# Stick-breaking attention: scaled queries split once, scores read by ScalarE, norms stored in columns

## Chip, cores and metric

The kernel runs on one core of a Trainium2 chip. A core has TensorE (PE; its loading of weights is listed apart as PEld), VectorE (DVE), ScalarE (ACT), GpSimd (POOL) and SyncE (SP), whose queue issues the DMAs here. The metric is the device time of one execution in microseconds; the median of the runs counts. All data are float32, and products of full accuracy are made from halves: every operand is split into a high part in the format fp32r and a rest (low part), and three matmuls, high by high, high by low and low by high, add up in PSUM.

## The reference

The model has two layers of width 1024 over 1024 positions: a gated DeltaNet layer and a layer with stick-breaking attention, each followed by a SwiGLU network and a gated embedding. The change lies in the attention alone. Its core:

```python
def sb_mixer(hn, k_sh, v_sh, w_q, q_norm, w_out):
    q = (hn @ w_q).reshape(b_, s_, SB_HEADS, SB_HEAD_DIM)
    q = (rms_norm(q, q_norm) * (SB_HEAD_DIM ** -0.5)).transpose(0, 2, 1, 3)
    o = stick_breaking(q, k_sh, v_sh)
    return o.transpose(0, 2, 1, 3).reshape(b_, s_, SB_WIDTH) @ w_out

def stick_breaking(q, k, v):
    ...
        z = jnp.einsum('bhtd,bhsd->bhts', q[:, :, t0:t1], k[:, :, :t1])
        mask = s_idx < t_idx
        log_not = jnp.where(mask, jax.nn.log_sigmoid(-z), 0.0)
        suffix = lax.cumsum(log_not, axis=3, reverse=True) - log_not
        log_w = jnp.where(mask, jax.nn.log_sigmoid(z) + suffix, -jnp.inf)
        outs.append(jnp.einsum('bhts,bhsd->bhtd', jnp.exp(log_w), v[:, :, :t1]))
```

There are 8 heads of 128 dimensions. The keys, too, are RMS-normalised per head and position.

## The kernel before

**Stages.** `whole` (line 2010) records DeltaNet, its tail, `attention` (line 1739) and its tail, one after the other. Activations lie transposed: 128 features on the partitions, 512 positions (a half, `hf` or `T`, 0 or 1) in the free dimension.

**The attention's work.** The dense part, `sb_dense` (line 1794), makes for each head the projections k, v and q of both halves, 24 matmuls each into a PSUM tile `mm`. After each one `sb_features` (line 1817) turns it into operands: ScalarE copies the tile to `ev` (two buffers); TensorE transposes it into a PSUM tile `z` (two buffers, shared with the scores); for k and q ScalarE sums the squares from there into `ms` (`msk`, `msq`), four numbers on each partition, DVE scales them, and GpSimd raises them to the power -0.5 (`rk`, `rq`, 128 x 4). DVE multiplies the keys by the gains `kq`, casts `ev` to the high part (`kh`, `qh`) and subtracts for the low part (`kl`, `ql`). The inverse norms of the keys stay as `rk`, one per partition of a score tile. Those of the queries are needed along the free dimension: TensorE transposes `rq` (4 rows of 128), DVE copies it to `rr`, a DMA stores it to `rD` in DRAM, and another loads it as a row into all 128 partitions, `rw`.

**The chains.** `sb_chains` (line 1875) spawns three generators for each head and half. `front` makes a score tile for each block of 128 keys, from the last block to the first (4 blocks in half 0, 8 in half 1; diagonal blocks have 128 to 512 columns): three matmuls into `z`, then DVE takes it out to `zs` and multiplies by `rk` and `rw` in one instruction (line 1908); ScalarE makes Abs, Exp and Ln into `t`; DVE adds the positive part; on diagonal blocks GpSimd masks (`select`); DVE splits `t` into `sh` and `sl`. `back` multiplies these by triangles of ones into the running sum `c`, and DVE subtracts it from `zs`. `weights` takes the exponential (ScalarE) and splits into `wh` and `wl`; `out` multiplies by the values `vh`, `vl` into `o`. At a half's end `o` is copied to an `ev` buffer, split and put to DRAM (`oD`), or straight into the operand tiles `x` of the output projection where those are there already (`spill`, line 1184).

**What sets the order.** Nothing on the chip does: every engine works through its instructions in the order in which they were recorded. The order comes from a planner, `Flow` (line 83), which runs all generators against a clock of its own with a cost for each instruction (line 114), buffers as slots (`slots`, `take`, `give`) and priorities (chains before features before dense work); the dense matmuls are its filling where no chain is ready. Its cost for a DMA (line 194) counts runs shorter than 128 elements as more data; its rule for GpSimd and DVE at their shared port (line 136) leaves the power out (line 143). A feature of q may be made up to four halves ahead of its use (line 1800). After the heads follows the output projection, `out_first` (line 1221) for half 0: its first two tiles are made together, all heads but the last first, then the last head. It is recorded into the last heads' chains as soon as `load_o` of half 0 is there.

Of the kernel before, what the change touches and what calls it, by code (L numbers as in the profile page):

```python
# [8 lines left out]
F32 = mybir.dt.float32  # L9
F32R = mybir.dt.float32r  # L10
AF = mybir.ActivationFunctionType
ALU = mybir.AluOpType
# [3 lines left out]
P = 128  # L16
# [3 lines left out]
H = 8  # L20
HW = 512
# [248 lines left out]
class Net:  # L270
    def __init__(self, tc, io, cp, act, wp, mm, dr):
# [7 lines left out]
        self.direct = set()  # L279
        self.early = []  # L280
        self.lead = 9.0
        self.slots = {tag: [0.0] * n for tag, n in {"mm": 2, "dn": 4, "u": 8, "tp": 3, "st": 2, "ca": 2, "zz": 1, "ou": 1, "vf": 2, "sg": 2, "xe": 2, "z": 2, "ev": 2, "pj": 3, "po": 1, "y": 3, "c": 2, "zs": 4, "t": 2, "hv": 2, "sl": 4, "wl": 2, "sh": 4, "wh": 2}.items()}
        self.banks = None
        nc = self.nc
        self.cst = cp.tile([P, 5, P], F32, name="cst")
# [1453 lines left out]
    def attention(self):  # L1739
        nc, io, tc, flow = self.nc, self.io, self.tc, self.flow  # L1740
        with ExitStack() as es:
            sp = es.enter_context(tc.tile_pool(name="as", bufs=2, reuse_waits="tile"))
            pp = es.enter_context(tc.tile_pool(name="ap", bufs=2, space=PSUM, reuse_waits="tile"))
# [23 lines left out]
                yield from self.normed(("n3", 1), self.r1, lambda k: hs[k], None, lambda: self.t(sp, "sh", bufs=4), "sh", lambda: self.give("zs"))  # L1767

            flow.spawn(second(), 0)
            for h in range(H):  # L1770
                for T in range(2):
                    self.sb_chains(h, T)
            yield from self.sb_dense()
            flow.spawn(self.late(), 4)
            yield lambda: ("tile", ("ol", 1, 0)) in flow.at
# [41 lines left out]
    def sb_features(self, n, h, hf, ps):  # L1817
        nc, sp, pp, flow, st = self.nc, self.sp, self.pp, self.flow, self.ast[h]
        yield from self.take("ev")
        yield  # L1820
        ev = self.t(sp, "ev")
        nc.scalar.copy(ev, ps)
        self.give("mm")
        a, b = (self.t(sp, n + p, dt=F32R, bufs=4 if n == "q" else 5) for p in "hl")
        st[n, hf] = (a, b)
        yield
        yield from self.take("z")
        pt = self.t(pp, "z")
        for c in range(4):
            nc.tensor.transpose(pt[:, c * P : (c + 1) * P], ev[:, c * P : (c + 1) * P], self.ident)  # L1830
        yield
        if n == "v":
            nc.scalar.copy(a, pt)
            yield
            nc.vector.tensor_tensor(b, pt, a.bitcast(F32), op=ALU.subtract)
            self.give("z", "ev")
            flow.mark(("ap", n, h, hf))
            return
        ms = self.t(sp, "ms" + n, (P, 4))
        for c in range(4):  # L1840
            nc.scalar.activation(self.junk, pt[:, c * P : (c + 1) * P], AF.Square, accum_out=ms[:, c : c + 1])
        self.give("z")
        src = ev
        if n == "k":
            nc.vector.tensor_scalar(ev, ev, self.kq, None, op0=ALU.mult)
        nc.vector.tensor_copy(a, ev)
        yield
        nc.vector.tensor_tensor(b, ev, a.bitcast(F32), op=ALU.subtract)
        yield
        self.give("ev")  # L1850
        nc.vector.tensor_scalar(ms, ms, 1.0 / P, EPS, op0=ALU.mult, op1=ALU.add)
        yield
        r = self.t(sp, "r" + n, (P, 4), bufs=4)
        nc.gpsimd.tensor_tensor(r, ms, self.nhalf[:, :4], op=ALU.pow)
        yield
        if n == "k":
            st["rk", hf] = r
            flow.mark(("ap", n, h, hf))
            return
        yield from self.take("z")  # L1860
        pr = self.t(pp, "z")
        nc.tensor.transpose(pr[:4, :P], r, self.ident)
        yield
        rr = self.t(sp, "rr", (4, P))
        nc.vector.tensor_copy(rr, pr[:4, :P])
        self.give("z")
        yield
        nc.sync.dma_start(self.rD[2 * h + hf], rr)
        yield
        rq = self.t(sp, "rw", bufs=3)  # L1870
        nc.sync.dma_start(rq, self.rD[2 * h + hf].rearrange("c p -> (c p)").unsqueeze(0).to_broadcast([P, HW]))
        st["rq", hf] = rq
        flow.mark(("ap", n, h, hf))

    def sb_chains(self, h, T):


        nc, sp, pp, flow, st = self.nc, self.sp, self.pp, self.flow, self.ast[h]
# [11 lines left out]
        def front():  # L1890
            yield lambda: all(flow.done(("ap", n, h, i)) for i in range(T + 1) for n in "kvq")
            yield from self.take("c")
            qh, ql = st["q", T]
            rq = st["rq", T]
            for j in range(jt, -1, -1):
                cols, dg, diag, js, n = geom(j)
                yield lambda: cnt["front"] - cnt["back"] < 3
# [5 lines left out]
                self.mmul(pz[:, cols], kh[:, js], ql[:, cols], False, False)  # L1903
                self.mmul(pz[:, cols], kl[:, js], qh[:, cols], False, True)
                yield
                yield from self.take("zs")
                z = self.t(sp, "zs", bufs=4)
                nc.vector.scalar_tensor_tensor(z[:, cols], pz[:, cols], rk[:, j % 4 : j % 4 + 1], rq[:, cols], op0=ALU.mult, op1=ALU.mult)
                self.give("z")
                yield  # L1910
                yield from self.take("t")
                t = self.t(sp, "t", bufs=2)
                nc.scalar.activation(t[:, cols], z[:, cols], AF.Abs)
                nc.scalar.activation(t[:, cols], t[:, cols], AF.Exp, scale=-1.0)
                nc.scalar.activation(t[:, cols], t[:, cols], AF.Ln, bias=1.0)
                yield
# [58 lines left out]
        def out():  # L1975
            po = None
# [13 lines left out]
            self.hdone[h] += 1  # L1990
            yield from self.take("ev")
            yield
            oe = self.t(sp, "ev")
            nc.scalar.copy(oe, po)
            yield
            if ("tile", ("ol", 1, T)) in flow.at:
# [95 lines left out]
```

## Time and profile before

| | |
|---|---|
| time, median of 3 runs | 2829.93 us (2829.88 to 2833.13) |
| the profiled execution | 2831.9 us, span 2830.2 us |
| granted TensorE clock, mean | 0.997 |
| attention, first transpose of `ev` to last `o` | 1523.4 to 2018 us |

The profile is that of one execution. Its timeline counts from the span's start; "busy" is the time in which an engine worked, "x" a number of instructions. All instructions carry the line of a helper (L64), so groups are told by their tiles, written output<-inputs without buffer numbers. The matmuls' ends are modelled and overlap the next start.

### The profile page before, as it was taken

The page shows a single profiled execution, that of the slowest core. Times are in us where ns is not written, and L with a number is a line of the kernel's source. Part 1 is how long each engine was busy: PE and PEld are TensorE (multiplying, and loading weights), DVE is VectorE, ACT ScalarE, POOL GpSimd, SP SyncE. Part 2 cuts the span into 40 slices and gives each one's busy share as a digit, 9 for nine tenths or more (in the row PEclk, how much of TensorE's full clock was granted, in tenths as well). Part 3 has the DMA queues.
Part 4 walks back from the last instruction along what each step waited for, and adds up shares of the span by engine and source line. Part 5 has one row for each costly group of instructions (what it writes and reads, how often), then busy time and mean ns, then how long its engine had stood idle before and what let it go on. Part 6 is the DMA issues. An engine that isn't in the chain of part 4 may idle for free.

```text
span 2830.2 us, 37782 instructions
## 1 busy us (share of the span) xinstructions
PE 2759.6 (98%) x13203; PEld 2271.2 (80%) x13203; DVE 2026.8 (72%) x3861; ACT 1276.1 (45%) x2567; POOL 881.6 (31%) x742
## 2 busy tenths in 40 slices
PE   8899999999999999999999999999999999999999
PEld 7687777888878888888877778887777888888777
DVE  7777787784685655477867888998796655557783
ACT  6646545553443433322345566666453333422241
POOL 0101110110056666543201222221027666734400
PEclk9999999999999999999999999999999999999999
DMA  4312221227624444587432111114524444477622
GB/s 144 130 60 78 68 73 63 77 84 247 218 79 157 145 151 149 198 313 305 152 129 95 49 46 64 60 46 160 178 91 143 155 143 155 152 287 284 266 97 104
DMA packets 165631, 395.89 MB, mean 140 GB/s; under 512 B 34048, under 2 KB 35392, under 8 KB 155968
## 3 DMA queue, kind: packets, MB, share of 16 engines
q1 hardware_dynamic: 165440, 393.48, 39.1%
q8 instruction: 104, 1.70, 0.3%
q14 instruction: 87, 0.71, 0.1%
HBM read 274.29 MB, written 119.11 MB: 139 GB/s over the span
## 4 chain that ended last, share of the span: by engine, by line
PE 74%; DVE 14%; ACT 2%; issue 2%; DMA 2%; POOL 1%; SPq 0%; POOLq 0%; DVEq 0%; ACTq 0%
PE dn L64 37%; PE mm L64 27%; PE tp L64 3%; PE z L64 2%; PE c L64 2%; PE o L64 2%; DVE yr L64 1%; DVE x L64 1%; DVE ca L64 1%; DVE wlo L64 1%; DVE xr L64 1%; DVE u L64 1%; DVE v L64 1%; DVE hx L64 1%; PE po L64 1%
## 5 line engine op out<-in xcount | busy, mean ns | idle before, releaser
L64 PE MATMUL mm<-x,whi 128*128 128x512 f32 x2880 | 951.2, 400 | 12.8 <-DVE x L64 7.9
L64 PEld LDWEIGHTS mm<-x,whi 128*128 128x128 f32 x2880 | 533.6, 189 | 115.0 <-DVE x L64 13.8
L64 PE MATMUL mm<-x,wlo 128*128 128x512 f32 x1440 | 573.7, 398 | 0.0
L64 PE MATMUL dn<-x,whi 128*128 128x512 f32 x1776 | 549.2, 390 | 2.1 <-DVE x L64 0.9
L64 POOL TENSOR_TENSOR wlo<-raw,whi 128x512 fp32r<-128x512 f32 x236 | 346.0, 1487 | 442.0 <-ACT whi L64 368.1
L64 ACT CAST whi<-raw 128x1024 fp32r<-128x1024 f32 x231 | 242.9, 1052 | 445.3 <-DVE raw L64 258.4
L64 PEld LDWEIGHTS dn<-x,whi 128*128 128x128 f32 x1776 | 333.1, 188 | 74.7 <-DVE x L64 3.3
L64 PE MATMUL dn<-x,wlo 128*128 128x512 f32 x888 | 345.8, 389 | 0.0
L64 PEld LDWEIGHTS mm<-x,wlo 128*128 128x128 f32 x1440 | 271.6, 189 | 47.5 <-issue 0.2
L64 PE MATMUL dn<-hx,whi 128*128 128x512 f32 x864 | 267.6, 391 | 0.5 <-DVE hx L64 0.4
L64 DVE TENSOR_TENSOR tt<-u,tt 128x512 fp32r<-128x512 f32 x140 | 144.4, 1031 | 82.0 <-ACT tt L64 82.0
L64 PEld LDWEIGHTS dn<-x,wlo 128*128 128x128 f32 x888 | 166.7, 188 | 34.4
L64 PEld LDWEIGHTS dn<-hx,whi 128*128 128x128 f32 x864 | 162.8, 189 | 35.5 <-DVE hx L64 1.3
L64 DVE TENSOR_TENSOR v<-v,dn 128x512 f32<-128x512 f32 x112 | 76.6, 685 | 155.2 <-PE dn L64 154.6
L64 DVE TENSOR_TENSOR wlo<-raw,whi 128x512 fp32r<-128x512 f32 x226 | 155.5, 698 | 33.9 <-ACT whi L64 33.8
L64 PE MATMUL dn<-hx,wlo 128*128 128x512 f32 x432 | 169.2, 392 | 3.4 <-POOL wlo L64 3.4
L64 POOL TENSOR_TENSOR wlo<-sw,whi 128x512 fp32r<-128x512 f32 x102 | 144.4, 1433 | 0.8 <-ACT whi L64 0.8
L64 ACT CAST tt<-u 128x512 fp32r<-128x512 f32 x140 | 85.1, 620 | 125.4 <-DMA yD<-tt 102.3
L64 DVE TENSOR_TENSOR E<-E,dn 128x512 f32<-128x512 f32 x132 | 90.0, 684 | 69.2 <-PE dn L64 66.9
L64 POOL TENSOR_TENSOR rs<-ms,nhalf 128x4 f32<-128x4 f32 x11 | 12.4, 1123 | 330.0 <-DVE ms L64 260.5
L64 DVE SCALAR_TENSOR_TENSOR ca<-xe,conv,ca 128x512 f32<-128x512 f32 x144 | 107.6, 749 | 6.2 <-ACT ca L64 6.0
L64 PE MATMUL dn<-y,whi 128*128 128x512 f32 x352 | 108.4, 389 | 0.0
(333 smaller groups left out, 5136.5 us busy)
## 6 DMA issues: line engine op xcount, KB each, us to landing
yD<-tt SPq DMA_DIRECT2D x296, 256.0 KB
x<-yD SPq DMA_DIRECT2D x58, 1024.0 KB
raw<-f_s SPq DMA_DIRECT2D x84, 512.0 KB
raw<-d_s SPq DMA_DIRECT2D x40, 512.0 KB
raw<-w_in SPq DMA_DIRECT2D x33, 512.0 KB
hx<-yD SPq DMA_DIRECT2D x16, 1024.0 KB
x<-oD SPq DMA_DIRECT2D x27, 512.0 KB
raw<-g_out SPq DMA_DIRECT2D x16, 512.0 KB
```

What stands on the lines that cost most here:

```text
L64: r = issue(*args, **kw)
```

## The change

Four edits, all in the attention.

1. The keys' gains are no longer multiplied in on DVE. ScalarE makes the high part with the gain as its scale, and DVE the low part in one instruction, `ev` times gain less high part, placed behind the power.
2. The queries' inverse norms are multiplied into `ev` before it is split. For that the norms are stored straight from `rq` (128 x 4), word by word into columns, and loaded as a row as before; the transpose on TensorE and the copy to `rr` are gone. DVE multiplies by the row, ScalarE casts, DVE subtracts. `ev` is held until then and has three buffers in place of two; `rw` has two in place of three.
3. A score tile is read from PSUM by ScalarE, twice: Abs with `rk` as scale into `t`, and Copy with that scale into `zs`. DVE's instruction is gone.
4. The last chains are spawned in another order: half 0 of head 7 ahead of half 1 of head 6.

```diff
@@ slots
-"z": 2, "ev": 2, "pj": 3
+"z": 2, "ev": 3, "pj": 3
@@ attention
-            for h in range(H):
-                for T in range(2):
-                    self.sb_chains(h, T)
+            chains = [(h, T) for h in range(H) for T in range(2)]
+            for h, T in chains[:-3] + [chains[-2], chains[-3], chains[-1]]:
+                self.sb_chains(h, T)
@@ sb_features
         self.give("z")
-        src = ev
         if n == "k":
-            nc.vector.tensor_scalar(ev, ev, self.kq, None, op0=ALU.mult)
-        nc.vector.tensor_copy(a, ev)
-        yield
-        nc.vector.tensor_tensor(b, ev, a.bitcast(F32), op=ALU.subtract)
-        yield
-        self.give("ev")
+            nc.scalar.activation(a, ev, AF.Copy, scale=self.kq)
+        yield
         nc.vector.tensor_scalar(ms, ms, 1.0 / P, EPS, op0=ALU.mult, op1=ALU.add)
         yield
         r = self.t(sp, "r" + n, (P, 4), bufs=4)
         nc.gpsimd.tensor_tensor(r, ms, self.nhalf[:, :4], op=ALU.pow)
-        yield
         if n == "k":
+            nc.vector.scalar_tensor_tensor(b, ev, self.kq, a.bitcast(F32), op0=ALU.mult, op1=ALU.subtract)
+            self.give("ev")
+            yield
             st["rk", hf] = r
             flow.mark(("ap", n, h, hf))
             return
-        yield from self.take("z")
-        pr = self.t(pp, "z")
-        nc.tensor.transpose(pr[:4, :P], r, self.ident)
-        yield
-        rr = self.t(sp, "rr", (4, P))
-        nc.vector.tensor_copy(rr, pr[:4, :P])
-        self.give("z")
-        yield
-        nc.sync.dma_start(self.rD[2 * h + hf], rr)
-        yield
-        rq = self.t(sp, "rw", bufs=3)
+        yield
+        nc.sync.dma_start(self.rD[2 * h + hf].rearrange("c p -> p c"), r)
+        yield
+        rq = self.t(sp, "rw")
         nc.sync.dma_start(rq, self.rD[2 * h + hf].rearrange("c p -> (c p)").unsqueeze(0).to_broadcast([P, HW]))
-        st["rq", hf] = rq
+        yield
+        nc.vector.tensor_tensor(ev, ev, rq, op=ALU.mult)
+        yield
+        nc.scalar.copy(a, ev)
+        yield
+        nc.vector.tensor_tensor(b, ev, a.bitcast(F32), op=ALU.subtract)
+        self.give("ev")
         flow.mark(("ap", n, h, hf))
@@ front
+                yield from self.take("t")
                 yield from self.take("zs")
+                t = self.t(sp, "t", bufs=2)
                 z = self.t(sp, "zs", bufs=4)
-                nc.vector.scalar_tensor_tensor(z[:, cols], pz[:, cols], rk[:, j % 4 : j % 4 + 1], rq[:, cols], op0=ALU.mult, op1=ALU.mult)
+                rj = rk[:, j % 4 : j % 4 + 1]
+                nc.scalar.activation(t[:, cols], pz[:, cols], AF.Abs, scale=rj)
+                nc.scalar.activation(z[:, cols], pz[:, cols], AF.Copy, scale=rj)
                 self.give("z")
-                yield
-                yield from self.take("t")
-                t = self.t(sp, "t", bufs=2)
-                nc.scalar.activation(t[:, cols], z[:, cols], AF.Abs)
                 nc.scalar.activation(t[:, cols], t[:, cols], AF.Exp, scale=-1.0)
```

Since the planner sets the order from its costs, every engine's order in the attention changes with this. Three places follow (the numbers in the names tell tiles apart and differ between the two kernels).

DVE behind the sum of squares of a query, half 0, in a middle head, before: the rows up to the instruction that first reads a score tile.

```order
L64 TENSOR_SCALAR msq_16790<-msq_16790 128x4
L64 TENSOR_TENSOR zs_16758<-zs_16758,c_16674 128x384
L64 CAST wh_16868<-zs_16756 128x512
L64 SCALAR_TENSOR_TENSOR t_16847<-zs_16830,t_16847 128x512
L64 SCALAR_TENSOR_TENSOR zs_16873<-z_16840,rk_16305,rw_16557 128x512
L64 TENSOR_TENSOR wlo_16806<-raw_16600,whi_16805 128x512
L64 TENSOR_TENSOR wl_16885<-zs_16756,wh_16868 128x512
L64 COPY rr_16895<-z_16891 4x128
```

The same place with the change, up to the multiplication by the row of norms, with the two rows behind it.

```order
L64 TENSOR_SCALAR msq_17779<-msq_17779 128x4
L64 SCALAR_TENSOR_TENSOR t_17794<-zs_17795,t_17794 128x512
L64 CAST wh_17824<-zs_17736 128x384
L64 TENSOR_TENSOR wl_17830<-zs_17736,wh_17824 128x384
L64 CAST sh_17832<-t_17794 128x512
L64 TENSOR_TENSOR sl_17839<-t_17794,sh_17832 128x512
L64 TENSOR_TENSOR zs_17795<-zs_17795,c_17682 128x512
L64 TENSOR_TENSOR raw_17348<-raw_17348,vec 128x1024
L64 TENSOR_TENSOR ev_17757<-ev_17757,rw_17847 128x512
L64 SCALAR_TENSOR_TENSOR t_17849<-zs_17850,t_17849 128x512
L64 CAST wh_17889<-zs_17795 128x512
```

The copy of the transposed norms and the reading of the score tile are gone; seven rows stand between the sum and `ev` times `rw`, which waits for the load of `rw`.

DVE behind the sum of squares of a key, in a middle head with the change, up to the first row that reads PSUM (`z`).

```order
L64 TENSOR_SCALAR msk_16568<-msk_16568 128x4
L64 SCALAR_TENSOR_TENSOR kl_16538<-ev_16535,kq,kh_16537 128x512
L64 SCALAR_TENSOR_TENSOR t_16593<-zs_16594,t_16593 128x512
L64 TENSOR_TENSOR raw_16197<-raw_16197,vec 128x1024
L64 CAST sh_16643<-t_16593 128x512
L64 SCALAR_TENSOR_TENSOR t_16609<-zs_16610,t_16609 128x128
L64 CAST wh_16650<-zs_16526 128x512
L64 TENSOR_TENSOR sl_16662<-t_16593,sh_16643 128x512
L64 TENSOR_TENSOR wl_16668<-zs_16526,wh_16650 128x512
L64 CAST sh_16672<-t_16609 128x128
L64 TENSOR_TENSOR wlo_16654<-raw_16197,whi_16653 128x512
L64 TENSOR_TENSOR vl_16638<-z_16657,vh_16637 128x512
```

Before, the first row on PSUM in such a place stands four rows behind the sum (`sl`, `t`, `wh`, then `zs` less `c`).

TensorE near the attention's end. Before: part of the stretch in which the chains of the last two heads stand without projection matmuls (`mm`) between them.

```order
L64 MATMUL c_18743<-sh_18991,triR 128x512
L64 MATMUL c_18743<-sl_19004,triR 128x512
L64 MATMUL o_18456<-wh_19002,vh_17656 128x512
L64 MATMUL o_18456<-wl_19008,vh_17656 128x512
L64 MATMUL o_18456<-wh_19002,vl_17657 128x512
L64 MATMUL z_19032<-qh_18754,kh_18543 128x256
L64 MATMUL z_19032<-ql_18755,kh_18543 128x256
L64 MATMUL z_19032<-qh_18754,kl_18544 128x256
L64 MATMUL c_19036<-sh_19028,triR 128x128
L64 MATMUL c_19036<-sl_19030,triR 128x128
L64 MATMUL o_18850<-wh_19039,vh_18326 128x512
```

With the change: the last product of head 7's half 0 (`o_18760`) and the matmuls on it (`mm_18791`, with the operand tile `x_18400` of the last two heads).

```order
L64 MATMUL mm_18824<-x_18400,wlo_18623 128x512
L64 MATMUL o_18760<-wh_18946,vh_18312 128x512
L64 MATMUL o_18760<-wl_18952,vh_18312 128x512
L64 MATMUL o_18760<-wh_18946,vl_18313 128x512
L64 MATMUL z_18960<-qh_18781,kh_18509 128x128
L64 MATMUL z_18960<-ql_18782,kh_18509 128x128
L64 MATMUL z_18960<-qh_18781,kl_18510 128x128
L64 MATMUL mm_18791<-x_18400,whi_18511 128x512
L64 MATMUL z_18982<-qh_18781,kh_18509 128x256
```

Projection matmuls stand between the chains here; behind the last product of half 0 three small score matmuls precede the first matmul on it.

More of the change, by code (lines that the diff above doesn't have):

```diff
@@ L281, in __init__ @@
         self.lead = 9.0
-        self.slots = {tag: [0.0] * n for tag, n in {"mm": 2, "dn": 4, "u": 8, "tp": 3, "st": 2, "ca": 2, "zz": 1, "ou": 1, "vf": 2, "sg": 2, "xe": 2, "z": 2, "ev": 2, "pj": 3, "po": 1, "y": 3, "c": 2, "zs": 4, "t": 2, "hv": 2, "sl": 4, "wl": 2, "sh": 4, "wh": 2}.items()}
+        self.slots = {tag: [0.0] * n for tag, n in {"mm": 2, "dn": 4, "u": 8, "tp": 3, "st": 2, "ca": 2, "zz": 1, "ou": 1, "vf": 2, "sg": 2, "xe": 2, "z": 2, "ev": 3, "pj": 3, "po": 1, "y": 3, "c": 2, "zs": 4, "t": 2, "hv": 2, "sl": 4, "wl": 2, "sh": 4, "wh": 2}.items()}
         self.banks = None
@@ L1820, in sb_features @@
         yield
-        ev = self.t(sp, "ev")
+        ev = self.t(sp, "ev", bufs=3)
         nc.scalar.copy(ev, ps)
@@ L1859, in sb_features @@
             return
-        yield from self.take("z")
-        pr = self.t(pp, "z")
-        nc.tensor.transpose(pr[:4, :P], r, self.ident)
         yield
-        rr = self.t(sp, "rr", (4, P))
-        nc.vector.tensor_copy(rr, pr[:4, :P])
-        self.give("z")
+        nc.sync.dma_start(self.rD[2 * h + hf].rearrange("c p -> p c"), r)
         yield
-        nc.sync.dma_start(self.rD[2 * h + hf], rr)
+        rq = self.t(sp, "rw")
+        nc.sync.dma_start(rq, self.rD[2 * h + hf].rearrange("c p -> (c p)").unsqueeze(0).to_broadcast([P, HW]))
         yield
-        rq = self.t(sp, "rw", bufs=3)
-        nc.sync.dma_start(rq, self.rD[2 * h + hf].rearrange("c p -> (c p)").unsqueeze(0).to_broadcast([P, HW]))
-        st["rq", hf] = rq
+        nc.vector.tensor_tensor(ev, ev, rq, op=ALU.mult)
[4 more added lines that the diff above has]
+        self.give("ev")
         flow.mark(("ap", n, h, hf))
@@ L1893, in front @@
             qh, ql = st["q", T]
-            rq = st["rq", T]
             for j in range(jt, -1, -1):
@@ L1992, in out @@
             yield
-            oe = self.t(sp, "ev")
+            oe = self.t(sp, "ev", bufs=3)
             nc.scalar.copy(oe, po)
```

## The prediction

> **What bounds the kernel now.** The page first, with the busy shares. Then the attention (1523 to 2018 us) by windows; the columns are PE, PEld, DVE, ACT and POOL busy (instructions), granted clock, DMA share, GB/s.
>
> ```profile
> span 2830.2 us, 37782 instructions
> PE 2759.6 (98%) x13203; PEld 2271.2 (80%) x13203; DVE 2026.8 (72%) x3861; ACT 1276.1 (45%) x2567; POOL 881.6 (31%) x742
> ```
> ```profile
> 1600.00:1700.00 100.00, 94.81 (x453) 77.91 (x453) 83.64 (x182) 61.57 (x150) 27.29 (x31) 0.97 0.14 49
> 1700.00:1930.00 230.00, 229.94 (x1148) 191.41 (x1147) 209.38 (x453) 157.78 (x382) 58.85 (x80) 1.00 0.16 56
> 1523.00:1970.00 447.00, 439.39 (x2168) 362.98 (x2168) 388.20 (x837) 291.02 (x720) 110.19 (x148) 0.99 0.20 70
> ```
>
> The reader is to see that TensorE is the bound, so an edit counts only by TensorE work that it removes or TensorE pauses that it ends or makes. Between 1700 and 1930 us there is hardly a pause, with DVE at 209.38 of 230 us (91%); the pauses lie before (94.81 of 100 us from 1600 on) and, as shown below, after 1976 us. The waits of TensorE in the attention come next (waited for: total, times, longest), then places in the timeline (start, duration, idle time before).
>
> ```profile
> PEld z L64 <- POOL rq L64: 8.5, 15, 2.5
> PE z L64 <- POOL rq L64: 4.1, 4, 2.1
> 1738.48 0.27 PE L64 MATMUL z<-cst,rq 128*4 128x128 f32 x1
> 1738.51 0.47 PE L64 MATMUL mm<-x,wlo 128*128 128x512 f32 x1
> 1738.82 0.39 PE L64 MATMUL mm<-x,whi 128*128 128x512 f32 x1
> 1764.04 0.40 PE L64 MATMUL mm<-x,whi 128*128 128x512 f32 x1
> 1764.44 0.27 PE L64 MATMUL z<-cst,rq 128*4 128x128 f32 x1
> 1613.63 0.27 PE L64 MATMUL z<-cst,rq 128*4 128x128 f32 x1 [2.08 <-POOL rq L64]
> 1614.25 0.63 PE L64 MATMUL z<-qh,kl 128*128 128x512 f32 x1
> 1617.63 0.40 PE L64 MATMUL mm<-x,whi 128*128 128x512 f32 x1
> 1617.86 0.40 PE L64 MATMUL mm<-x,wlo 128*128 128x512 f32 x1
> ```
>
> Durations of matmuls overlap, so I count from start to start: 0.23 us for a full 512 columns (1617.63 to 1617.86). A transpose of the norms and the matmul behind it take 0.34 (1738.48 to 1738.82), so the transpose costs 0.11. Ahead of the one at 1764.44 TensorE stood 0.17 (0.40 less 0.23). And after the pause of 2.08 us eight matmuls from 1614.25 to 1617.63 take 3.38 us in place of 1.84, 0.42 each.
>
> The long pauses have one root, a GpSimd power that is itself late:
>
> ```profile
> L64 POOL TENSOR_TENSOR rq<-msq,nhalf x16: 1007/1073/3902, 1535.9 to 1964.0; 128x4 f32<-128x4 f32 x16
> 1655.40 3.12 POOL L64 TENSOR_TENSOR rk<-msk,nhalf 128x4 f32<-128x4 f32 x1 [0.68 <-DVE msk L64]
> 1657.23 0.42 DVE L64 CAST sh<-t 128x512 fp32r<-128x512 f32 x1
> 1658.47 0.40 PE L64 MATMUL mm<-x,wlo 128*128 128x512 f32 x1
> 1660.35 0.50 PE L64 MATMUL z<-qh,kh 128*128 128x512 f32 x1 [1.48 <-DVE zs L64]
> 1665.17 0.48 PE L64 MATMUL mm<-x,whi 128*128 128x512 f32 x1
> 1976.80 0.22 PE L64 MATMUL z<-qh,kh 128*128 128x128 f32 x1
> 1986.71 0.44 PE L64 MATMUL mm<-x,whi 128*128 128x512 f32 x1
> ```
>
> A power of the queries' norms takes 1.07 us at the median and 3.9 at most; that of a key in the second row took 3.12. It ends at 1658.52, 0.87 us after DVE ran out of work (1657.65): GpSimd got through only behind it. The Trainium skill (GPSIMD Engine Reference, section Key points) says that GpSimd shares its SBUF interfaces with VectorE and contends with DVE instructions that have two SBUF inputs; the trace agrees, 3.12 against 1.07 us. TensorE paid for that one with 1658.47 to 1665.17: 6.7 us for 14 matmuls (twelve of 512 columns and two of 128) that take 2.9 at the usual steps, 3.8 lost. The last two rows bound the stretch without projection matmuls near the end: 9.9 us for 29 matmuls, 4.0 at the usual steps (0.23 for 512 columns, in proportion for fewer), so 5.9 lost.
>
> **The change part by part.** The sum is made against the profiled execution, 2831.9 us (span 2830.2 and 1.7 around it), 2.0 above the median of 2829.93.
>
> ```profile
> L64 DVE SCALAR_TENSOR_TENSOR zs<-z,rk,rw 128x512 f32<-128x512 f32 (+3 forms) x96 | 58.2, 611 | 6.5 <-PE z L64 5.5 <-issue 0.9
> L64 DVE TENSOR_SCALAR ev<-ev,kq 128x512 f32<-128x512 f32 x16 | 7.7, 480 | 2.5 <-PE z L64 2.4
> L64 DVE CAST kh<-ev 128x512 fp32r<-128x512 f32 x16 | 6.8, 428 | 0.5
> L64 DVE COPY rr<-z 4x128 f32<-4x128 f32 x16 | 4.4, 273 | 2.6 <-PE z L64 2.6
> L64 DVE TENSOR_TENSOR ql<-ev,qh 128x512 fp32r<-128x512 f32 x16 | 11.0, 686 | 0.2
> L64 ACT ACTIVATE t<-zs 128x512 f32<-128x512 f32 (+3 forms) x96 | 50.0, 521 | 55.9 <-DVE zs L64 55.5
> L64 ACT ACTIVATE t<-t 128x512 f32<-128x512 f32 x96 | 60.8, 633 | 3.1
> L64 ACT COPY ev<-mm 128x512 f32<-128x512 f32 x48 | 28.1, 585 | 46.1 <-PE mm L64 42.4 <-DMA oD<-ev 3.6
> L64 ACT ACTIVATE ca<-xe,conv 128x512 f32<-128x512 f32 x48 | 34.7, 723 | 1.2
> ```
>
> DVE loses 58.2 + 7.7 + 4.4 and the casts of k and q (2 x 6.8), 83.9 us, and gets 16 multiplications at 0.686, 11.0. Of 388.2 us in 447 it keeps about 315 (71%). This gives nothing by itself, since TensorE did not wait while DVE was at 91%.
>
> ScalarE gets two readings of each score tile for one. No row shows one of 512 columns from PSUM with a scale per partition; from PSUM a copy takes 585 (633 from SBUF without a scale, 723 with one), so 48 ns less and 90 more: 521 - 48 + 90 = 563 on average. The bounds are 521 and 611. Twice 96 of them are 108 us less the 50.0 of today, 58 more, and 32 casts at 0.63 to 0.72 about 21: 79 us. ScalarE goes from 291 to 370 of 447 us (83%), less than DVE bears now: nothing on the path, hidden under the projection matmuls; if that cover fails, a late score tile stops TensorE.
>
> **TensorE's gains.** (a) 16 transposes at 0.11: 1.8. (b) Their waits: four of 4.1 in all, the eleven others of the 15 at 0.17, 1.9: 6.0 together (8.5 by the weight loads' row is the upper end, 4.1 the lower). (c) The slow steps after 1614.25: 1.5. (d) The stretch from 1658.47: 3.8, which goes only if no power is held up at such a place. (e) In the new order projections stand between the last heads' chains, so the stretch with its 5.9 goes. But the first two output tiles now end on head 7's last product, with two small score matmul groups between: its copy (0.59), four activations of 128 columns (0.25 each, an estimate from 0.633 for 512), the cast (0.63) and the hand-overs make some 2.6 us, with 0.4 of matmuls to cover it, and 1.5 of slow steps follow as in (c). I take 3.7 lost there, so a gain of 2.2 (bounds 0 and 5.9). Sum: 15.3.
>
> **What it adds for TensorE.** (f) The scaled queries wait on DVE for the row of norms, which comes back through DRAM.
>
> ```profile
> 1707.77 0.26 SPq L64 DMA_DIRECT2D rD<-rr  x1
> 1708.94 0.34 SPq L64 DMA_DIRECT2D rw<-rD  x1
> 1740.70 0.27 SPq L64 DMA_DIRECT2D rD<-rr  x1
> 1743.14 0.34 SPq L64 DMA_DIRECT2D rw<-rD  x1
> 85.59 1.80 SPq L64 DMA_DIRECT2D Ld<-LT  x4
> 88.66 0.59 SPq L64 DMA_DIRECT2D Ls<-Ld  x1
> DMA packets 144, 0.26 MB, mean 90 GB/s; under 512 B 16, under 2 KB 16, under 8 KB 144
> ```
>
> From the store's issue to the load's it is 1.17 us, 2.44 behind a weight load. The store becomes 512 words in place of 4 rows of 512 bytes. Nearest to it are the four stores at 85.59, 1024 short rows, read back 3.07 us after the first issue. So 1.2 to 3.1; I take 2.0, between, since there are half as many pieces. The Trainium skill (DMA: Bandwidth & Descriptors, Rules for kernel authors) advises against this form: a last dimension that is not contiguous becomes one descriptor per element. By 3.1 the round trip would be 1.1 longer than I count. The load that is issued at 1539.1 us moved all of its 144 packets by 1542.0 (the last row, the DMA view of that window), 2.9. So from the power's end to the row: 2.0 + 2.9 = 4.9 after, 0.7 + 1.2 + 2.9 = 4.8 before (0.7 for the transpose and the copy, 0.27 each, with their hand-overs); then multiply, cast and difference, 2.0. The query is some 2 us later; by the code it is made up to four features ahead, and three buffers for "ev" in place of two bear the longer hold: nothing on the path from that. But in the order of the change DVE has some 4 us of work between the sum of the squares and the multiplication (first halves, shown above with the change) and 6 in second halves, and power and round trip need 1.1 + 4.9. DVE covers the difference by the waits that it has anyway (29% of its time), and stands as soon as power or store is late, with the casts of scores and weights queued behind, for which TensorE waits.
>
> (g) Behind a sum on DVE there are now fewer readings of PSUM at which GpSimd gets through: in the order, twelve of sixteen keys' sums have 2.7 us or more of SBUF work behind them (at 0.6 for two inputs of 512 columns, 0.35 a cast, 1.1 the gains), and three had. At 71% DVE will mostly have gaps. I count (f) and (g) together as three holds in place of today's, at 0 to 3.8 each; I take 1.7, since the keys' norms have no direct waiter on TensorE: 5.1 (bounds 0 and 15, four at 3.8).
>
> Net: 15.3 - 5.1 = 10 us less. 2831.9 - 10 = 2822 in a profile, **2820 by the median**.
>
> **The rivals.** A measurement of this kernel tells about 0.2% (5.7 us) from no change.
>
> 1. The whole gain: no new hold, and the end's 5.9 us go whole: 15.3 + 3.7 = 19, 2811. For it speaks that TensorE had no pause with DVE at 91%; against it the long runs on DVE and the new wait. 0.20.
>
> 2. The holds take it back: half of the twelve keys meet a gapless DVE, six at 1.7, and (e) gives nothing: 15.3 - 2.2 - 10.2 = 3 less, 2827. This is the mechanism of the row at 1655.40 made more frequent. (The rule of the Trainium skill on the shared SBUF interfaces, GPSIMD Engine Reference, Key points, points this way.) Also that the change does little, with the wait for the norms only moved from TensorE to DVE, ends here. 0.24.
>
> 3. Slower: DVE stands at the multiplication in every feature of q. It decides at a store of over 2.0 us, or of any length behind a held power (2.0 to 2.8 late). With 2.0 us lost by TensorE in each of 13 queries, 26 - 15 = 11 more, 2841. For it speaks the store of 2.44 behind a weight load; against it, that this load stands behind every other query at most and that TensorE's order has projections between. 0.12.
>
> **How the numbers follow.** My forecast, a gain of 6 to 14, holds 0.44, rival 1 0.20, rival 2 0.24, rival 3 0.12. The range from 2809 to 2832 takes in rivals 1 and 2 and the bounds of (e) and (b), and leaves out most of rival 3 and the far end of rival 1. Faster by over 0.2%: 0.64; within: 0.24; slower: 0.12.
>
> **What would show it.** Right: no wait of TensorE for the queries' power, DVE near 71% and ScalarE near 83% between 1523 and 1970 us, the store read back after about 2.0 us, projections in the last stretch with one pause of 2 to 3 us. Wrong: DVE idle for the row of norms at its multiplication for over a microsecond each time (rival 3), powers of over 2.5 us behind the keys' sums with slow steps of TensorE after them (rival 2), or score tiles waiting for ScalarE, which no term here counts.

## The result and the profile after

The changed kernel takes 2960.09 us (median of 4 runs, 2955.97 to 2967.12), the kernel before 2831.53 us (4 runs, 2829.88 to 2837.38): ratio **1.0453**, 95% interval 1.0434 to 1.0473. It is slower by some 129 us, where the forecast was 2820 us.

First the page of the changed kernel, then the three windows that were shown of before (PE, PEld, DVE, ACT and POOL busy with instructions, granted clock, DMA share, GB/s).

```profile
span 2958.3 us, 37695 instructions
PE 2795.4 (94%) x13187; PEld 2297.1 (78%) x13187; DVE 1972.0 (67%) x3717; ACT 1333.5 (45%) x2695; POOL 863.5 (29%) x742
DMA packets 173951, 395.88 MB, mean 134 GB/s; under 512 B 42432, under 2 KB 43712, under 8 KB 164288
```
```profile
1600.00:1700.00 100.00, 81.39 (x365) 66.03 (x364) 61.45 (x126) 61.06 (x145) 17.00 (x26) 0.88 0.21 40
1700.00:1930.00 230.00, 195.88 (x912) 160.97 (x911) 145.11 (x305) 147.57 (x353) 37.23 (x64) 0.92 0.16 44
1523.00:1970.00 447.00, 374.82 (x1728) 306.93 (x1727) 268.23 (x557) 272.24 (x671) 73.29 (x121) 0.90 0.20 47
```

No engine is near its limit here: TensorE fell from 439 to 375 of 447 us, and DVE and ScalarE, which were to stand at 71 and 83%, are both near 60%. The granted clock is 0.90. The last product `o` of the attention starts at 2154.3 us, before at 2028.7 (the 2018 us in the table of the kernel before is the last reading of a score tile): of the 128 us between the two profiled executions 126 lie in the attention. The waits of the attention, to 2150 us (who waits for whom: total, times, longest), name the place:

```profile
DVE ev L64 <- DMA rw<-rD: 119.7, 16, 10.9
ACT qh L64 <- DVE ev L64: 107.1, 16, 10.6
PE o L64 <- DVE wh L64: 54.6, 9, 9.5
PE c L64 <- DVE sl L64: 22.9, 4, 7.8
PE z L64 <- ACT qh L64: 20.5, 4, 6.8
```

In the 16 queries DVE stands 7.5 us on average (119.7 / 16) at the multiplication of `ev` by the row of norms; ScalarE stands behind it at the cast; and TensorE stands for whatever was queued on DVE behind that multiplication: weights `wh`, split `sl`, the query itself. One such place in the timeline (start, duration, what):

```profile
1600.25 1.01 POOL L64 TENSOR_TENSOR rq<-msq,nhalf 128x4 f32<-128x4 f32 x1 [1.88 <-DVE msq L64]
1601.29 0.37 SPq L64 DMA_DIRECT2D rD<-rq  x1
1609.64 0.32 SPq L64 DMA_DIRECT2D rw<-rD  x1
1614.89 0.69 DVE L64 TENSOR_TENSOR ev<-ev,rw 128x512 f32<-128x512 f32 x1 [7.18 <-DMA rw<-rD]
1615.62 0.62 ACT L64 CAST qh<-ev 128x512 fp32r<-128x512 f32 x1 [5.73 <-DVE ev L64]
1616.30 0.47 PE L64 MATMUL z<-qh,kh 128*128 128x128 f32 x1 [4.49 <-ACT qh L64]
1618.60 0.63 PE L64 MATMUL z<-ql,kh 128*128 128x512 f32 x1
1619.03 0.63 PE L64 MATMUL z<-qh,kl 128*128 128x512 f32 x1
1619.45 0.63 PE L64 MATMUL mm<-x,wlo 128*128 128x512 f32 x1
```

The power is not late: 1.01 us, at once. But from the store's issue to the load's it is 8.35 us (1601.29 to 1609.64), and another 5.2 until the row is there. TensorE pauses 4.49 us, and afterwards its matmuls start 0.43 us apart (1618.60, 1619.03, 1619.45) in place of 0.23. The landings of the stores (first row) and of the loads (second), from the view of the tiles (minimum, median, maximum):

```profile
DMA to landing us min/median/max: 8.2/8.5/10.9
DMA to landing us min/median/max: 3.3/4.7/5.6
```

The DMA view of the same stretch, 1601.0 to 1609.6 us (40 slices of 0.215 us; a digit is the busy share in tenths), shows that the words are not under way for so long:

```profile
DMA  0000037000000000000000000000000000000000
DMA packets 528, 0.00 MB, mean 0 GB/s; under 512 B 528, under 2 KB 528, under 8 KB 528
```

All 528 packets (each of 4 bytes; 512 are the words) start between 0.9 and 1.3 us after the issue; then the DMA engines show nothing for seven microseconds, until the landing is reported. So the time lies behind the engines, at the DRAM or on the way to it: in e10 below 512 words leave a tile of the same form, only their places in DRAM are 64 bytes apart, and they land after 1.8 us. The Trainium skill (DMA: Bandwidth & Descriptors, section Anatomy of one DMA) says, for DMAs issued by GpSimd, that the semaphore can't fire before the last byte is confirmed in the target memory; these here are issued by SyncE, and the trace agrees with such a wait, 7 us of it.

That is the leading theory: the word-wise store lands 8.5 us after its issue, DVE stands for it, and everything else follows. The rivals: the new wait as such or ScalarE's second reading (then a short store helps little), the planner's placing of the multiplication (then the long store is harmless if placed later), and a harm of the words to the DMA queue.

### The profile page after: what moved, and what is told of

The parts are those of the page before. It is cut to its first block, busy times and chain, and to the rows that moved or that the text cites. A ratio compares the mean times of both kernels' runs of the same rounds, so it can differ in the third digit from the quotient of the medians.

```text
span 2958.3 us, 37695 instructions
## 1 busy us (share of the span) xinstructions
PE 2795.4 (94%) x13187; PEld 2297.1 (78%) x13187; DVE 1972.0 (67%) x3717; ACT 1333.5 (45%) x2695; POOL 863.5 (29%) x742
## 5 line engine op out<-in xcount | busy, mean ns | idle before, releaser
L64 PE MATMUL mm<-x,whi 128*128 128x512 f32 x2880 | 962.6, 404 | 13.7 <-DVE x L64 7.2
L64 PEld LDWEIGHTS mm<-x,whi 128*128 128x128 f32 x2880 | 540.5, 191 | 116.8 <-DVE x L64 12.5
```

What stands on the lines that cost most here:

```text
L64: r = issue(*args, **kw)
```

## The experiments

Ratios are to the kernel before, run beside each on the same chip. e4, e5 and e10, one run each, are there for the landings and stand with their times below.

| kernel | time, us | ratio (95% interval) |
|---|---|---|
| the change | 2960.09 | 1.0453 (1.0434 to 1.0473) |
| e1 row store | 2822.78 | 0.9957 (0.9942 to 0.9972) |
| e2 multiplication planned later | 2845.70 | 1.0044 (1.0029 to 1.0059) |
| e3 word store in the kernel before | 2910.32 | 1.0271 (1.0253 to 1.0288) |
| e6 runs of 16 bytes, same order | 2824.14 | 0.9969 (0.9958 to 0.9980) |
| e7 row store, old order of chains | 2824.24 | 0.9974 (0.9965 to 0.9983) |
| e8 order of chains alone | 2832.62 | 1.0003 (0.9994 to 1.0012) |
| e9 every fourth position | 2825.26 | 0.9976 (0.9968 to 0.9985) |
| e11 row store, scores by DVE | 2827.05 | 0.9979 (0.9970 to 0.9988) |

### e1: the store by rows again

```diff
-        nc.sync.dma_start(self.rD[2 * h + hf].rearrange("c p -> p c"), r)
+        yield from self.take("z")
+        pr = self.t(pp, "z")
+        nc.tensor.transpose(pr[:4, :P], r, self.ident)
+        yield
+        rr = self.t(sp, "rr", (4, P))
+        nc.vector.tensor_copy(rr, pr[:4, :P])
+        self.give("z")
+        yield
+        nc.sync.dma_start(self.rD[2 * h + hf], rr)
```

> The changed kernel with one thing undone: the norms go through TensorE's transpose and DVE's copy and are stored as 4 rows of 512 bytes, as before. Theory A (the store of single words lands 8.4 us after its issue, and DVE stands for it): the row is there some 7 us earlier, DVE's stand of 7.2 us in each query falls under 1.5 us, and the time is 2815 to 2845 us. Rival B (not the store's form but the new wait as such, or ScalarE with two readings of each score tile): DVE still stands 3 us or more per query, or score tiles wait for ScalarE, and the time stays above 2880 us.

2822.78 us: theory A. The whole loss is gone, 137 us or 8.6 per query, and a gain of 0.43% is left (interval 0.28 to 0.58). Its window, and two of its waits:

```profile
1523.00:1970.00 447.00, 444.46 (x2211) 367.58 (x2210) 349.09 (x735) 344.36 (x849) 98.94 (x153) 1.00 0.22 72
```
```profile
DVE ev L64 <- DMA rw<-rD: 6.0, 7, 1.7
PE z L64 <- POOL rq L64: 1.5, 4, 0.6
```

TensorE is busy for 444.46 us (439.39 before); DVE stands 6.0 us in all at seven multiplications, and hardly any of that reaches TensorE.

### e2: the word store, with the multiplication planned later

```diff
@@ Flow.issued, eng == "dma"
             end = self.rings
+            if any(x.name.startswith("rD") and x.space == DRAM for x in outs):
+                end = t + 7.6
+            if any(x.name.startswith("rD") and x.space == DRAM for x in ins):
+                end = t + 4.0
```

> The changed kernel with its word-wise store, but the planner is told that this store ends 7.6 us and the row's load 4.0 us after its start, so that it puts DVE's multiplication some 10 us later. Theory A1 (the store's length costs only because DVE's program has the multiplication too early): DVE's stands fall under 1.5 us each and the time is 2815 to 2850 us. Rival A2 (the length itself costs: the three buffers of ev are held 10 us longer and the features behind them come late): DVE does not stand, but TensorE or ScalarE waits for ev, and the time is above 2870 us.

2845.70 us, inside A1's range, but not quite by its picture. The landing of the stores (minimum, median, maximum) and DVE's wait for the row:

```profile
DMA to landing us min/median/max: 8.8/10.3/11.4
```
```profile
DVE ev L64 <- DMA rw<-rD: 22.6, 12, 4.1
```

The planner's own rule puts the end of the word-wise store 1.8 us after its start on an idle queue (1.1, and 0.7 for words counted as 128 times their bytes). The landing is 10.3 us here, longer than the 7.6 that the planner was told, and DVE still stands 1.9 us in twelve queries, over the 1.5 expected. So placement buys back about 115 of the 137 us with the slow store kept; the other 23 stay. It was not run with a still later placement.

### e3: the word store alone, in the kernel before

```diff
-        yield from self.take("z")
-        pr = self.t(pp, "z")
-        nc.tensor.transpose(pr[:4, :P], r, self.ident)
...
-        nc.sync.dma_start(self.rD[2 * h + hf], rr)
+        nc.sync.dma_start(self.rD[2 * h + hf].rearrange("c p -> p c"), r)
```

> The kernel before with the word-wise store alone (transpose and copy to rr gone; the row is used, as before, where DVE takes a score tile out). Theory A (the harm is in who waits for the store): the row is first read by a score tile a good way behind the query, so most of the 7 us are covered; 16 transposes go, 1.8 us; the time is 2815 to 2850 us. Rival C (the store harms by itself, since the words keep the DMA queue busy and weight loads come late): above 2880 us, with TensorE waiting for weights.

2910.32 us: a miss for theory A as I had put it, and the time that C gave, but not by C's way. No wait of TensorE for weights is among its waits; those that matter are others:

```profile
ACT t L64 <- DVE zs L64: 124.6, 47, 11.2
DVE zs L64 <- DMA rw<-rD: 70.9, 13, 9.6
PE z L64 <- ACT ev L64: 22.2, 5, 8.3
```

In 13 queries DVE stands 5.5 us (70.9 / 13) at a score tile that takes the row; ScalarE waits for these score tiles, and TensorE for the copies `ev` queued on ScalarE behind them. So the claim that queries are made well ahead of their use does not hold in this order. It does not hold in the kernel before either: by its trace and its program the row is first read 3.8 to 6.9 us after its load's issue in 13 of the 16 queries (11.9 to 13.1 us in the other three), and the load takes some 2.9 of that. The first query, for one, has its load issued at 1539.1 us and its first score tile at 1543.6. The place of the wait differs, the mechanism is the one of the changed kernel.

### e4 and e5: forms of the store

The kernel before with one more store of `rq` per query into DRAM of its own, in eight forms (e4); then with a load of one word behind it, for which SP has to wait (e5).

```diff
+    def probe(self, u, r):
+        d, k = self.rP[u][:, :, 0], u % 8
+        if k in (0, 5, 6):
+            return d.rearrange("c p -> p c"), r
...
+        form, src = self.probe(2 * h + hf, r)
+        self.tc.nc.sync.dma_start(form, src)
+        self.tc.nc.sync.dma_start(sp.tile([1, 1], F32, tag="pb", name=self.nm("pb"), bufs=2), self.rP[2 * h + hf][0, :1, :1])
```

> The kernel before with one store more per query, read by nobody, issued behind the row's load; eight forms, each twice: 512 words as the change stores them, 256 words (two columns), 128 words (one), 128 runs of 16 bytes side by side, 256 words from 64 partitions, 512 words each 64 bytes from the next, 512 words each 512 bytes from the next, 16 words. Theory D (each word that lands in a line shared with others costs a fixed time at the DRAM): landing in proportion to the words, about 8.4, 4.8, 3.0, 3.0, 4.8 us, under 2.5 us for the two spread forms, 1.5 for 16 words. Rival E (a cost of each descriptor, wherever it lands): the spread forms take 8.4 us too. Rival F (any store of short pieces lands late by a fixed time): all forms 7 us or more. Time of the kernel within 10 us of before.

> The kernel before with the additional stores of the form test, and behind each a load of one of its words into a tile that nobody uses, so that SP waits for the store and the time from the store's issue to that load's issue is its landing. Theory D (a fixed time at the DRAM for each piece that shares a line or a row with others): 8.4 us for 512 words side by side, about 4.8 for 256, 3.0 for 128 and for 128 runs of 16 bytes, under 2.5 for the spread forms, 1.2 to 1.5 for 16 words. Rival E (a cost of each descriptor wherever it lands): the spread forms take 8.4 as well. Rival F (short pieces land late by a fixed time): all 7 us or more. The kernel's time is of no interest here, some 10 to 60 us over before, since SP and its weight loads wait.

e4 (2844.42 us, one run) settled nothing on the landings: nobody waits for those stores, so the trace gives no landing. e5 (2839.85 us, one run) does. From the store's issue to the load's, both samples of each form, behind the row's load of 256 KB (which the 16 words show to cost some of the first microseconds):

| form | us |
|---|---|
| 512 words, as the change stores them | 8.31, 10.08 |
| 256 words, two columns | 8.69, 7.88 |
| 128 words, one column | 7.97, 7.33 |
| 256 words, from 64 partitions | 7.28, 7.72 |
| 128 runs of 16 bytes side by side | 3.02, 2.99 |
| 512 words, each 64 bytes from the next | 3.30, 4.26 |
| 512 words, each 512 bytes from the next | 3.22, 4.51 |
| 16 words | 2.23, 2.72 |

D's proportion to the words fails (a quarter of the words takes 7.3 to 8.0 us), E fails by the spread forms, F by four of the eight. What the long forms share is words 4 bytes apart, in long rows.

### e6: runs of 16 bytes, the order of all engines unchanged

```diff
-        nc.sync.dma_start(self.rD[2 * h + hf].rearrange("c p -> p c"), r)
+        nc.sync.dma_start(self.rD[2 * h + hf].rearrange("c p -> (c p)").rearrange("(p c) -> p c", c=4), r)
@@ Flow.issued, eng == "dma"
-            n *= max(1, P // run)
+            n *= P if any(x.name.startswith("rD") and x.space == DRAM for x in outs) else max(1, P // run)
```

> The changed kernel, every engine's order word for word the same, but the 512 words are stored partition by partition, 128 runs of 16 bytes; the row that comes back has the norms in another order, so the values of the queries are not the reference's. Theory A (DVE's stand is the store's landing) with D: the landing is 3.0 us in place of 8.4, DVE's stand 7.2 - 5.4 = 1.8 us per query, and of the 137 us that separate the changed kernel from the one with the row store about 30 are left: 2835 to 2865 us. If the landing is otherwise, the time lies on the line between 2823 us at 1.2 and 2960 us at 8.4 us, no higher. Rival G (something else than the store's landing, such as the load that comes back or the words' number of bytes): landing short and the time still above 2900 us.

2824.14 us, lower than expected, because the landing is lower still. Landings of the store and of the load, and DVE's wait:

```profile
DMA to landing us min/median/max: 1.4/1.9/3.4
DMA to landing us min/median/max: 3.2/4.0/6.7
```
```profile
DVE ev L64 <- DMA rw<-rD: 10.8, 7, 4.3
```

This is the cleanest of the runs: each engine has the same instructions in the same order as in the changed kernel, the same bytes go to DRAM, and 136 us are gone. The landing fell by 6.6 us (8.5 to 1.9) and the time by 8.5 us per query (136 / 16), so in this order each microsecond of the landing cost about 1.3. The load's landing fell by only 0.7. G has fallen.

### e7 and e8: the order of the last chains

e7 is e1 with the chains spawned as before; e8 is the kernel before with the new order.

```diff
@@ e7, against e1
-            for h, T in chains[:-3] + [chains[-2], chains[-3], chains[-1]]:
+            for h, T in chains:
```

> The changed kernel with the row store and with the chains spawned as before (half 1 of head 6 ahead of half 0 of head 7). By the prediction's term (e) the other order is worth 2.2 us, with 0 and 5.9 as bounds: 2825 us, 2822 to 2829, with projection-free pauses of TensorE after 1976 us back. Rival: the gain of the row store kernel comes from the order alone and this one falls back to 2831 us or more.

> The kernel before with the new order of the last chains alone. By term (e): 2.2 us less than before, 0 to 5.9, so 2826 to 2832 us. Rival: nearly the whole gain of the row store kernel, 10 us or more; other rival: nothing, or slower, since the first output tiles then end on head 7's last product with nothing to cover it.

The order alone gives a ratio of 1.0003 (0.9994 to 1.0012), between 1.7 us less and 3.4 us more: nothing that can be seen. With the row store the old order gives 0.9974, the new one 0.9957, and the intervals overlap. Neither the 2.2 us of term (e) nor a loss is shown. From 1970 to 2030 us TensorE is busy for 57.15 us of 60 before and 56.36 with the order alone, so no gain; with the row store it is 57.42 in the old order and 58.83 in the new.

### e9: every fourth position

```diff
-            nc.tensor.transpose(pt[:, c * P : (c + 1) * P], ev[:, c * P : (c + 1) * P], self.ident)
+            cols = ev.rearrange("f (p c) -> f c p", c=4)[:, c] if n == "q" else ev[:, c * P : (c + 1) * P]
+            nc.tensor.transpose(pt[:, c * P : (c + 1) * P], cols, self.ident)
-        nc.sync.dma_start(self.rD[2 * h + hf].rearrange("c p -> p c"), r)
+        nc.sync.dma_start(self.rD[2 * h + hf].rearrange("c p -> (c p)").rearrange("(p c) -> p c", c=4), r)
```

> The changed kernel, complete: the four transposes of a query's tile take every fourth position (position 4p+c lands on partition p of tile c), so that the 128 runs of 16 bytes, stored partition by partition, lie in the order of the positions and the row that comes back is right. By the run with 16-byte runs at the unchanged order: the store is read back after 1.4 to 3 us, DVE stands under 1 us per query, and the time is 2816 to 2828 us, below the kernel before. Rival: reading with a stride of 16 bytes makes the 64 transposes slower on TensorE, over 0.11 us each beyond today, and the time is 2830 us or more.

2825.26 us, ratio 0.9976: 0.15 to 0.32% faster than before, and without the transpose of the norms and the copy. It is not faster than e1, although it has 16 transposes fewer. Its stores land after 2.4 us at the median and DVE stands for the row longer than in e1 (15.5 us in all against 6.0):

```profile
DVE ev L64 <- DMA rw<-rD: 15.5, 10, 3.2
```

### e10: the distance of the words

The keys' norms `rk` are stored in addition, and one word of them is loaded back, in the features of k, where SP's queue is mostly empty.

```diff
+        self.rP = [dr.tile([4, P, (1, 2, 4, 8, 16, 1, 1, 1)[u % 8]], F32, name=f"rP{u}") for u in range(NU)]
...
+            to, src = self.probe(u, r)
+            self.tc.nc.sync.dma_start(to, src)
+            self.tc.nc.sync.dma_start(sp.tile([1, 1], F32, tag="pb", name=self.nm("pb"), bufs=2), self.rP[u][0, :1, :1])
```

> The kernel before with a store of the keys' norms and a load of one word behind it, in each feature of k, where SP's queue has little else; eight forms, each twice: 512 words 4, 8, 16, 32 and 64 bytes apart (so 16, 8, 4, 2 and 1 in 64 bytes), 128 runs of 16 bytes, 128 words 4 bytes apart, 32 words 4 bytes apart. Theory H (writes that fall into the same short stretch of DRAM follow one another, and stretches go side by side, so that the number of words in a stretch counts and not the number of words): 8.3, some 4.5, 2.5, 1.7, 1.4 us for the five distances, 1.4 for the runs, and 7 to 8 us for 128 and for 32 words alike. Rival I (the number of words counts): 128 words take a third of 512, 32 words under 2 us. Time of the kernel within 20 us of before.

The first sample of 512 words at 4, 8 and 64 bytes and of the runs of 16 bytes, in SP's timeline (store, then the load that waited for it):

```profile
1531.16 0.37 SPq L1860 DMA_DIRECT2D rP<-rk  x1
1539.72 0.29 SPq L1861 DMA_DIRECT2D pb<-rP  x1
1554.02 0.37 SPq L1860 DMA_DIRECT2D rP<-rk  x1
1558.64 0.23 SPq L1861 DMA_DIRECT2D pb<-rP  x1
...
1635.05 0.37 SPq L1860 DMA_DIRECT2D rP<-rk  x1
1636.88 0.24 SPq L1861 DMA_DIRECT2D pb<-rP  x1
1669.29 0.32 SPq L1860 DMA_DIRECT2D rP<-rk  x1
1670.69 0.23 SPq L1861 DMA_DIRECT2D pb<-rP  x1
```

| form | us, two samples |
|---|---|
| 512 words, 4 bytes apart | 8.56, 8.47 |
| 512 words, 8 bytes apart | 4.62, 3.75 |
| 512 words, 16 bytes apart | 2.65, 2.38 |
| 512 words, 32 bytes apart | 1.79, 2.95 |
| 512 words, 64 bytes apart | 1.83, 1.80 |
| 128 runs of 16 bytes side by side | 1.40, 3.35 |
| 128 words, 4 bytes apart | 7.50, 7.68 |
| 32 words, 4 bytes apart | 4.00, 3.93 |

The same 512 words land after 8.5 us at 4 bytes and after 1.8 at 64; up to 16 bytes each doubling of the distance takes away more than half of what lies above the shortest landing, 1.4 us. So the distance decides for 512 words, as H says, and I fails with 128 words at 7.5. But 32 words at 4 bytes take 4.0 where H had 7 to 8: the number counts too, and between 32 and 128 words the landing nearly doubles. A rule in one number does not follow from these forms, and H's picture of short stretches is not shown beyond that. The kernel took 2845.66 us in its one run.

### e11: the row store, with the scores still taken by DVE

```diff
@@ front, against e1
-                nc.scalar.activation(t[:, cols], pz[:, cols], AF.Abs, scale=rj)
-                nc.scalar.activation(z[:, cols], pz[:, cols], AF.Copy, scale=rj)
+                nc.vector.tensor_scalar(z[:, cols], pz[:, cols], rk[:, j % 4 : j % 4 + 1], None, op0=ALU.mult)
...
+                nc.scalar.activation(t[:, cols], z[:, cols], AF.Abs)
```

> The kernel with the row store, but DVE takes the scores out of PSUM (one input and a scale), and ScalarE makes Abs from there, as before; the queries are still scaled first. Theory J (what gains is that the wait for the row has left the score tiles, so that TensorE no longer waits behind late powers): 2820 to 2828 us as with ScalarE. Rival K (what gains is DVE's relief, 74 to 80% busy in place of 91%): 2829 us or more, with TensorE's waits for the norms' transposes and slow steps back.

2827.05 us, ratio 0.9979: in the range of theory J, under that of K. The wait of TensorE for the queries' power is down to 0.3 us although DVE is at 386 of 447 us:

```profile
1523.00:1970.00 447.00, 444.18 (x2201) 365.83 (x2200) 386.49 (x815) 310.43 (x759) 108.11 (x150) 1.00 0.22 74
```
```profile
PE z L64 <- POOL rq L64: 0.3, 1, 0.3
```

So a gain of 0.21% (interval 0.12 to 0.30) comes without ScalarE's readings, about half of e1's 0.43% by the medians and most of e7's 0.26%. Whether the readings add to it is open, since the intervals of e11 and e1 touch. That it is the row's move off the score tiles that gains is argued: the keys' gains (the first edit) are changed in e11 too and were not run alone.

## Why the prediction was wrong

**The step that failed** is the store in (f): "So 1.2 to 3.1; I take 2.0, between, since there are half as many pieces." It measured 8.5 us at the median, 8.2 at the least. The upper bound came from stores of 1024 rows of 128 bytes, counted by pieces; but the number of pieces alone is not what costs. 512 words land after 1.8 us when they are 64 bytes apart (e10), and 128 runs of 16 bytes after 1.9 at the median in e6 (1.4 at the least, near the row store's 1.2). Words side by side are another case, of which no row of before was an example, so both ends of the bound lay on one side. The rule of the Trainium skill that I cited there (DMA: Bandwidth & Descriptors, Rules for kernel authors: one descriptor per element where the last dimension isn't contiguous) pointed at the right place, but gives no price for the landing; in the trace the packets have all started 1.3 us after the issue, and the other 7 us come behind them. A figure on the same page (Specifications: below 512 bytes the DMA does read-modify-write) doesn't separate the cases either: runs of 16 bytes and words 64 bytes apart are below it too, and land after 1.9 and 1.8 us at 512 words; no run here shows what the DMA does with them.

**The second step that failed** is the cover: "by the code it is made up to four features ahead ... nothing on the path from that". The code only sets a limit there; e3, and the trace of the kernel before, show the row used soon after it is back. At the place shown the row came 13.6 us after the power's end (1601.26 to 1614.89) against the 4.9 of the forecast, 8.7 late: 6.4 of it by the store (8.35 for 2.0) and 2.3 by the load (5.2 for 2.9). DVE stood 7.2, and the kernel lost 8.6 per query over all.

**Rival 3 was right in its mechanism** ("DVE stands at the multiplication in every feature of q") and in its place, DVE's queue with the casts of scores and weights behind it, and in its point of decision, a store over 2.0 us. Only its price was off, for the same term: 2.0 us in 13 queries, 26 us, where 8.6 us in 16 were lost, 137 us. Its chance of 0.12 rested on the same bound.

**Apart from the store the sum came out near, in part by luck.** With the row store, and so with the transposes back, the change gives 2822.78 us, ratio 0.9957, 8 to 16 us less than before; the forecast was 10 less. But 4.0 us of gains that no run shows, (a) and (e), stand in the sum against 5.1 of losses, (f) and (g), that were not paid; (b), (c) and (d) alone make 11.3. The terms one by one:

- (a) The 16 transposes at 0.11: e9 has them away and is no faster than e1. Not shown.
- (b), (c), (d) The waits behind the powers: they shrink, also where the transposes stay. TensorE waited 4.1 us for the queries' power before, 1.5 in e1, 0.3 in e11. The longest power of a query was 3.9 us before, 1.5 in e1. Between 1600 and 1700 us, where (c) and (d) lie, TensorE is busy for 94.81 us before, 99.71 in e1 and 99.09 in e11. By e11 it does not take ScalarE's readings for that.
- (e) The order of the last chains: nothing that could be measured (e8), where 2.2 us were counted.
- (g) The keys' powers are held at times, and TensorE does not wait for them. Power of the keys, before, then e1 (nanoseconds: minimum, median, maximum):

```profile
L64 POOL TENSOR_TENSOR rk<-msk,nhalf x16: 1007/1184/3118, 1528.3 to 1943.3; 128x4 f32<-128x4 f32 x16
```
```profile
L64 POOL TENSOR_TENSOR rk<-msk,nhalf x16: 1007/1431/3262, 1530.6 to 1942.2; 128x4 f32<-128x4 f32 x16
```

  The median rose from 1.18 to 1.43 us, as the longer runs on DVE let expect, but no matmul waits for this power in e1. The 5.1 us of (f) and (g) were not paid there.

**ScalarE's share.** The estimate of 563 ns for a score tile was near; in the changed kernel the two readings take

```profile
L64 ACT ACTIVATE t<-z,rk 128x512 f32<-128x512 f32 (+3 forms) x96 | 55.7, 580 | 63.2 <-PE z L64 55.2 <-DVE sl L64 4.3 <-DVE zs L64 1.5
L64 ACT ACTIVATE zs<-z,rk 128x512 f32<-128x512 f32 (+3 forms) x96 | 55.3, 576 | 1.3 <-DVE wl L64 1.3
```

580 and 576. In e1 ScalarE is at 344 of 447 us (77%, forecast 83) and DVE at 349 (78%, forecast 71). DVE's forecast took the 58.2 us of all 96 score tiles off a window that holds 87 of them (52.3 us), and e1 has the copy to `rr` back. ScalarE as the bound, a risk that no term counted, did not occur.

## What to carry to other kernels

A store that breaks a tile into single words side by side in DRAM is not priced by its bytes or its number of pieces alone; give each partition a run of 16 bytes, or transpose first, and look at the landing, not at the packets. When a DMA's result goes to an engine that works in order, ask when that engine reaches the use, and count the whole round trip up to it; a planner that has the price wrong will put the wait where it hurts. A limit in the code on how far ahead something may be made does not say how far ahead it is made: look in the trace. When the only bound for a new cost comes from operations of another kind, its upper end is a guess, and the range should say so.

## What the runs showed of the hardware that was not expected

- 512 words of 4 bytes to DRAM land 8.5 us after the issue when they lie side by side, and 1.8 us after it when they are 64 bytes apart; side by side, their packets start within 0.4 us at the place shown of the change's trace.
- Behind such a store a load crawls. In e4, between 1543.8 and 1549.0 us, a weight load runs with the DMA engines busy and little moved:

```profile
DMA packets 34, 0.14 MB, mean 27 GB/s; under 512 B 0, under 2 KB 0, under 8 KB 34
q1 hardware_dynamic: 34, 0.14, 62.5%
```

  62.5% of the engines' time for 27 GB/s. The change's trace has another case: a weight load of 512 KB issued at 1640.42 us, half a microsecond behind a store, lands 12.5 us after its issue, where the median of the weight loads whose landing the trace gives is 4.1. That it is the words still being written that hold it is argued from the times, not shown by a run of its own. In e3 and in the change TensorE did not wait for such loads.
- The load of the row, the same in both kernels, took 2.9 us to its last packet before, and 4.7 at the median to its landing in the change, which is reported some 0.3 us behind the last packet; in e6 it is 4.0. The load begins later rather than running slower: at 1609.64 us in the change the first of its packets starts 2.7 us after the issue, at 1539.1 us before 1.0. Why was not settled.
